# Low part of some weight tiles of the first down projection formed by an accumulating DMA

## The chip, the core and the metric

The kernel runs on one core of a Trainium2 chip. The metric is the device time of one execution in microseconds (us). Five engines work side by side on a core, each with its own queue of instructions in program order, and wait for one another by semaphores: TensorE (PE; the loading of its stationary operand is listed as PEld), VectorE (DVE), ScalarE (ACT), GpSimd (POOL) and SyncE (SP), which here only issues DMAs. Sixteen DMA engines move data between HBM and the on-chip memory SBUF. TensorE accumulates into PSUM.

## The reference

Two layers of a decoder over 256 tokens of width 2048: a retention mixer in layer 0, a convolution module in layer 1, and in each layer a SwiGLU feed-forward and a per-layer embedding, with norms around each. The change touches the last product of the feed-forward of layer 0, `... @ w_down`:

```python
def swiglu(hn, w_gate, w_up, w_down):
    return (jax.nn.silu(hn @ w_gate) * (hn @ w_up)) @ w_down

f = swiglu(rms_norm(h, g_ffn_pre[i]), ffn_w_gate[i], ffn_w_up[i], ffn_w_down[i])
h = h + rms_norm(f, g_ffn_post[i])
```

All data are f32. The hidden width is 5632.

## The kernel before

Every product of activations and weights is computed from parts. A number is split into a high part, its value rounded to TensorE's float32r, and a low part, the number minus the high part. A product is then the sum of three: high by high, high by low and low by high (`mm3`, lines 120 to 122).

`gemm` (line 124) computes a block of 256 tokens by 512 output columns. Tokens are two tiles of 128 (`tt`), each with an accumulator in PSUM. K runs in steps of 256 rows (`su`), and for every step `wload` (line 75) prepares one weight tile of 128 partitions by 2 x 512 numbers, 512 KB:

1. SP loads it into a stage tile `st` (line 68); there are four stage buffers.
2. ACT casts it to the high part `wh` (line 79); there are eight buffers.
3. DVE subtracts, `wl = st - wh` (line 84); there are eight buffers of `wl` too.

PE then does 12 products per tile: two halves of 128 rows, two token tiles, three parts. The engines take tiles in program order, so a cast waits for PE to have finished the tile eight before, and a load waits until the stage tile four before has been read by both ACT and DVE. In the ordinary form of `gemm` both token tiles are served inside the loop over K. With `outer=True` the token tiles are the outer loop and the eight weight tiles stay for both; this form has its own call of `wload` (line 146).

`ffn` (line 565) goes through the hidden width in three groups of 3, 4 and 4 blocks of 512. For each group it computes gate ("fg") and up ("fu") blocks, forms the hidden activations, and then multiplies them with the group's rows of `w_down` ("fd") for each of four blocks `c` of 512 output columns. In a group of four blocks, K of "fd" is 2048: eight weight tiles per block, 32 per group. The results of the second group are added to what is there by DVE (line 601); those of the third go through `make_final` (lines 528 and 530). Only the last block of the third group has `outer=True`.

GpSimd does little: a power of a column of 128 numbers for each norm (`rstd_from`, line 170), and some memsets. No DMA is issued from it.

Of the kernel before, what the change touches and what calls it, by code (L numbers as in the profile page):

```python
# [17 lines left out]
P = 128  # L18
# [11 lines left out]
NFREQ = BLOCK_LEN // 2  # L30
# column offsets of the conv transform's matrices, each as a high and a low part side by side
DFT_AT = {}
# [9 lines left out]
def block_kernel(ctx: ExitStack, tc: tile.TileContext, x, p, positions, w_in, w_out, w_pw1, b_pw1,  # L42
# [15 lines left out]

# [1 line left out]
    def t512(name):  # L60
# [13 lines left out]

    def wload(src, shape=(2, CW)):
        st = stage.tile([P] + list(shape), F32, tag="st", name="st")
        wdma(st, src)
        wh = wpool.tile([P] + list(shape), F32R, tag="wh", name="wh")
        nc.scalar.copy(wh, st)  # L79
        wl = wpool.tile([P] + list(shape), F32R, tag="wl", name="wl")  # L80
        with ExitStack() as es:
            if held:
                es.enter_context(tc.issue_after(held[0].ins))
            nc.vector.tensor_tensor(wl, st, wh.bitcast(F32), op=ALU.subtract)  # L84
        return wh, wl
# [19 lines left out]
    def split_to(act, q, tt, src):  # L105
        """src: [P, 4, 128] f32 (psum or sbuf), channel on partition."""
        hi, lo = act.quarter(q)
        a = nc.scalar.copy(hi[:, tt], src)  # L108
        b = nc.vector.tensor_tensor(lo[:, tt], src, hi[:, tt].bitcast(F32), op=ALU.subtract)  # L109
        return a, b  # L110

    def transpose4(src, n=4):
        """src: [P, n*128] f32 in sbuf -> psum tile [P, n, 128]"""
        tp = tpp.tile([P, n, P], F32, tag="tp", name="tp")
        for j in range(n):
            nc.tensor.transpose(tp[:, j, :], src[:, j * P:(j + 1) * P], ident)
        return tp
# [5 lines left out]

    def gemm(act, w, k0, c0, nkt, name, outer=False, hooks=None, on_done=None, hooks1=None):
        """acc[tt] = act.T @ w[k0:k0+128*nkt, c0:c0+512]"""
        hooks, hooks1 = hooks or {}, hooks1 or {}
        acc = [acc_tile(f"{name}{tt}") for tt in range(TT)]
        if not outer:
            for su in range(nkt // 2):
                wh, wl = wload(wsrc(w, k0 + su * 256, c0))  # L130
                for r in range(2):
                    kt = su * 2 + r
                    for tt in range(TT):
                        xh, xl = act.get(tt, kt)
                        mm3(acc[tt], xh, xl, wh[:, r, :], wl[:, r, :], kt == 0, kt == nkt - 1)
                if su in hooks:
                    hooks[su]()
            if on_done:
                for tt in range(TT):
                    on_done(tt, acc[tt])  # L140
        else:
            ws = []
            for tt in range(TT):
                for su in range(nkt // 2):
                    if tt == 0:
                        ws.append(wload(wsrc(w, k0 + su * 256, c0)))
                    wh, wl = ws[su]
                    for r in range(2):
                        kt = su * 2 + r
                        xh, xl = act.get(tt, kt)  # L150
                        mm3(acc[tt], xh, xl, wh[:, r, :], wl[:, r, :], kt == 0, kt == nkt - 1)
                    at = (hooks, hooks1)[tt]
                    if su in at:
                        at[su]()
                if on_done:
                    on_done(tt, acc[tt])
        return acc

    def rstd_from(ssq, n):
        """ssq: [P, m] partial sums of squares -> [P, 1] rstd"""  # L160
        m = ssq.shape[-1]
        if m > 1:
            s = small.tile([P, 1], F32, tag="s1", name="s1")
            nc.vector.tensor_reduce(s, ssq, axis=mybir.AxisListType.X, op=ALU.add)
        else:
            s = ssq
        v = small.tile([P, 1], F32, tag="s2", name="s2")
        nc.vector.tensor_scalar(v, s, 1.0 / n, EPS, op0=ALU.mult, op1=ALU.add)
        r = small.tile([P, 1], F32, tag="rstd", name="rstd", bufs=8)
        nc.gpsimd.tensor_tensor(r, v, neghalf, op=ALU.pow)  # L170
        return r
# [11 lines left out]

# [1 line left out]
    ident = const.tile([P, P], F32, name="ident")  # L185
# [7 lines left out]
    def preload(func):  # L193
        """has ACT's table loaded ahead of its use"""
        nc.scalar.activation(warm, neghalf, func)

    preload(AF.Silu)

    # what opens the chain comes first: the first gain, then x and the first weights by turns
    cols = const.tile([P, 96], F32, name="cols")  # L200
# [38 lines left out]

# [1 line left out]
    def prenorm_quarter(act, q, tt, src, gcol):  # L241
# [11 lines left out]
    def next_in(engine, i):  # L253
        """keeps an engine to the order in which the opening is traced"""
        if engine in turn:
            tc.add_manual_dep(i.ins, turn[engine].ins.name,
                              mybir.DependencyInfo(mybir.DependencyClass.NoSync, mybir.DependencyReason.DATA),
                              reason="opening")
        turn[engine] = i

    def opening(acc):
        """first product: x is transposed and split by quarters, in step with the weights"""
        fs = {}
# [49 lines left out]
    def rotary_tables():  # L313
# [35 lines left out]
        for a, c in ((a1, cs[2]), (a2, cs[1]), (a2, cs[0]), (a1, cs[1])):  # L349
# [4 lines left out]
            nc.vector.tensor_tensor(tacc, tacc, q, op=ALU.add)  # L354
        # the largest product, up to 2**29, sheds its whole turns in two steps
        nc.vector.tensor_scalar(q, a1, cs[0], None, op0=ALU.mult)
# [102 lines left out]
    def later(f):  # L459
        """behind the opening on DVE"""  # L460
        def g():
            with tc.issue_after(turn["dve"].ins):
                f()
        return g
# [17 lines left out]
    for h in range(HEADS):  # L482
# [15 lines left out]
        gemm(xa, wi, 0, 8192 + CW * h, NKT, "g", hooks=hk2, on_done=hd.g_done)  # L498
        # q and k columns of the head share one accumulator
        acc = [acc_tile(f"qk{tt}") for tt in range(TT)]  # L500
# [11 lines left out]

    # second half of the output projection, post norm and residual
    def post_setup():
        return [ssq_tile() for _ in range(TT)]

    def make_final(c, ssqs, gvec, after, bias=None, first=False):
        """evacuation of the last K group of chunk c; after(tt, rstd) runs at the last chunk"""
        gt = bcast_chunk(gvec, c)
# [43 lines left out]

# [1 line left out]
    def ffn(layer, s_hid, after):  # L565
# [6 lines left out]
        for gi, n in enumerate(groups):  # L572
# [20 lines left out]
            for c in range(NC):  # L593
                last = gi == len(groups) - 1
                if last:
                    done = make_final(c, ssqs, g_ffn_post[layer], after)
                elif gi == 0:
                    done = first_group_done(c)
                else:
                    def done(tt, ps, c=c):  # L600
                        nc.vector.tensor_tensor(y[tt, c], ps, y[tt, c], op=ALU.add)
                gemm(hid, wd, f0 * CW, c * CW, 4 * n, "fd", outer=(last and c == NC - 1),
                     on_done=done, hooks={1: pend} if c == 0 else None)
            f0 += n
        es.close()

    # operand sets: retention 0 and 1, ffn0 0 with hidden 1, ple0 0, conv 1, pw2 0, ffn1 1 with hidden 0, ple1 1
    pa = [Act(0, "pa0"), Act(1, "pa1")]
# [7 lines left out]

# [1 line left out]
    def ple(layer, after):  # L618
# [44 lines left out]

# [1 line left out]
    ca = Act(1, "ca")  # L665
# [11 lines left out]
    def conv(after):  # L677
# [17 lines left out]
        def mm3c(ps, name, rows, hi, lo, first, last):  # L695
            """constant stationary, data moving"""
            nc.tensor.matmul(ps, lhsT=dmat(name, rows, 0), rhs=hi, start=first, stop=False)
# [3 lines left out]
        class Chunk:  # L701
# [26 lines left out]
            def taps(self):  # L728
                """transform of the taps of the chunk's channels"""
                c = self.c  # L730
# [115 lines left out]
def _constants():  # L846
    """tables that depend on shapes alone: rotary frequencies and the decay masks of the heads"""
    inv = (10000.0 ** (-np.arange(P, dtype=np.float64) / P)).astype(np.float32)
# [11 lines left out]
def _short(a):  # L860
    """the nearest numbers of 12 significant bits"""
    m, e = np.frexp(a)
    return np.ldexp(np.rint(m * 4096.0) / 4096.0, e)


def _transform():
    """matrices of an odd-frequency Fourier transform of BLOCK_LEN points, in which the 31 taps and a block of
    128 tokens convolve without wrapping round"""
    th = 2.0 * np.pi * (np.arange(NFREQ) + 0.5) / BLOCK_LEN
# [44 lines left out]
```

## Time and profile before

| | us |
|---|---|
| median of the two runs | 2788.08 |
| the two runs | 2787.88 and 2788.28 |
| span of the profiled execution | 2785.6 |

The span runs from the first to the last instruction of one profiled execution; the time of a run also holds what lies around it. Shares on the profile's page are of the span. A wait is put down to the engine or the DMA whose signal came last. A row `<-` names what a tile is made from or, in a list of waits, who was waited for.

### The profile page before, as it was taken

How to read it: one execution, taken by the hardware profiler on the slowest of the kernel's cores; microseconds unless marked ns; L12 is line 12 of the kernel's file. 1: busy time of each engine (PE TensorE's matmuls, PEld its weight loads, DVE VectorE, ACT ScalarE, POOL GpSimd, SP SyncE). 2: the span in 40 equal slices, each digit the busy share in tenths (PEclk: the TensorE clock that was granted, in tenths of full speed). 3: DMA queues.
4: the chain of work that ended last, by engine and by line, in shares of the span. 5: the costliest groups of instructions: out<-in, count | busy, mean ns of one | idle time of the engine just before them, and what ended most of it. 6: DMA issues, size and time to landing. Idle time of an engine off the chain costs nothing.

```text
span 2785.6 us, 31985 instructions
## 1 busy us (share of the span) xinstructions
PE 2731.3 (98%) x12258; PEld 2251.0 (81%) x12258; DVE 1546.5 (56%) x1673; ACT 1247.0 (45%) x1490; POOL 39.4 (1%) x48
## 2 busy tenths in 40 slices
PE   8999999999999999999999989899999999999998
PEld 7888888888888888888887867668888888888877
DVE  7655545555655445545456566566554455454564
ACT  5444444444454444444445543355444443444453
POOL 0000000000000000000000000000000000000000
PEclk9999999999999999999999999999999999999999
DMA  8655555556565666566555555436655665665553
GB/s 270 192 179 183 182 193 183 181 178 212 169 209 189 195 190 189 189 195 189 190 201 178 179 192 164 154 111 211 214 188 191 193 188 192 191 188 193 202 180 122
DMA packets 288730, 521.76 MB, mean 187 GB/s; under 512 B 17900, under 2 KB 52556, under 8 KB 288576
## 3 DMA queue, kind: packets, MB, share of 16 engines
q1 hardware_dynamic: 288576, 519.71, 57.4%
q8 instruction: 96, 1.57, 0.2%
q14 instruction: 58, 0.48, 0.0%
HBM read 517.55 MB, written 2.10 MB: 187 GB/s over the span
## 4 chain that ended last, share of the span: by engine, by line
PE 92%; DVE 3%; DMA 3%; ACT 1%; issue 0%; POOL 0%; SPq 0%; DVEq 0%; POOLq 0%; ACTq 0%
PE fu L122 6%; PE fu L120 6%; PE fu L121 6%; PE fg L122 6%; PE fg L121 6%; PE fg L120 5%; PE fd L121 5%; PE fd L120 5%; PE fd L122 5%; PE v L121 2%; PE v L122 2%; PE v L120 2%; PE g L120 2%; PE g L122 2%; PE g L121 2%; PE qk L121 2%
## 5 line engine op out<-in xcount | busy, mean ns | idle before, releaser
L84 DVE TENSOR_TENSOR wl<-st,wh 128x1024 fp32r<-128x1024 f32 x944 | 1153.5, 1224 | 1075.4 <-ACT wh L79 1072.9
L79 ACT CAST wh<-st 128x1024 fp32r<-128x1024 f32 x944 | 993.0, 1053 | 1285.0 <-PE fu L122 270.2
L120 PE MATMUL fg<-wh,h_fa 128*128 128x512 f32 x704 | 275.4, 392 | 0.5 <-ACT h_fa L108 0.5
L121 PE MATMUL fg<-wl,h_fa 128*128 128x512 f32 x704 | 274.4, 390 | 0.4 <-DVE wl L84 0.4
L120 PE MATMUL fd<-wh,h_hid 128*128 128x512 f32 x704 | 274.8, 390 | 0.0
L122 PE MATMUL fg<-wh,l_fa 128*128 128x512 f32 x704 | 274.5, 390 | 0.0
L122 PE MATMUL fd<-wh,l_hid 128*128 128x512 f32 x704 | 274.2, 389 | 0.0
L121 PE MATMUL fd<-wl,h_hid 128*128 128x512 f32 x704 | 274.1, 389 | 0.0
L120 PE MATMUL fu<-wh,h_fa 128*128 128x512 f32 x704 | 273.9, 389 | 0.0
L121 PE MATMUL fu<-wl,h_fa 128*128 128x512 f32 x704 | 273.9, 389 | 0.0
L122 PE MATMUL fu<-wh,l_fa 128*128 128x512 f32 x704 | 273.9, 389 | 0.0
L121 PEld LDWEIGHTS fg<-wl,h_fa 128*128 128x128 f32 x704 | 132.2, 188 | 27.9 <-DVE wl L84 1.1
L122 PEld LDWEIGHTS fg<-wh,l_fa 128*128 128x128 f32 x704 | 132.2, 188 | 27.6 <-DVE l_fa L109 0.4
L120 PEld LDWEIGHTS fg<-wh,h_fa 128*128 128x128 f32 x704 | 132.2, 188 | 27.4 <-ACT h_fa L108 0.7
L121 PEld LDWEIGHTS fu<-wl,h_fa 128*128 128x128 f32 x704 | 132.2, 188 | 27.5
L122 PEld LDWEIGHTS fu<-wh,l_fa 128*128 128x128 f32 x704 | 132.2, 188 | 27.4
L122 PEld LDWEIGHTS fd<-wh,l_hid 128*128 128x128 f32 x704 | 132.2, 188 | 27.4
L120 PEld LDWEIGHTS fu<-wh,h_fa 128*128 128x128 f32 x704 | 132.2, 188 | 27.3
L120 PEld LDWEIGHTS fd<-wh,h_hid 128*128 128x128 f32 x704 | 132.2, 188 | 27.2
L121 PEld LDWEIGHTS fd<-wl,h_hid 128*128 128x128 f32 x704 | 132.2, 188 | 27.0
L120 PE MATMUL v<-wh,h_x 128*128 128x512 f32 x256 | 101.0, 396 | 0.0
L121 PE MATMUL v<-wl,h_x 128*128 128x512 f32 x256 | 100.3, 392 | 0.5 <-DVE wl L294 0.5
(235 smaller groups left out, 3819.7 us busy)
## 6 DMA issues: line engine op xcount, KB each, us to landing
st<-in_ffn_w_gate_dram SPq DMA_DIRECT2D x176, 512.0 KB, 3.6
st<-in_ffn_w_up_dram SPq DMA_DIRECT2D x176, 512.0 KB, 3.6
st<-in_ffn_w_down_dram SPq DMA_DIRECT2D x176, 512.0 KB, 3.5
st<-in_ret_w_in_dram SPq DMA_DIRECT2D x128, 512.0 KB, 3.7
st<-in_conv_w_pw_dram SPq DMA_DIRECT2D x96, 512.0 KB, 3.8
st<-in_ret_w_in_dram SPq DMA_DIRECT2D x128, 256.0 KB, 2.8
st<-in_ret_w_out_dram SPq DMA_DIRECT2D x64, 512.0 KB, 3.6
st<-in_ple_w_gate_dram SPq DMA_DIRECT2D x64, 512.0 KB, 4.9
```

Of the source, the lines that this page charges most:

```text
L79: nc.scalar.copy(wh, st)
L84: nc.vector.tensor_tensor(wl, st, wh.bitcast(F32), op=ALU.subtract)
L120: nc.tensor.matmul(ps, lhsT=xh, rhs=wh, start=first, stop=False)
L121: nc.tensor.matmul(ps, lhsT=xh, rhs=wl, start=False, stop=False)
L122: nc.tensor.matmul(ps, lhsT=xl, rhs=wh, start=False, stop=last)
```

## The change

`wload` gets an argument `by_dma`. Where it is set, ACT writes the negative of the stage tile, rounded, into `wl`, and GpSimd issues a DMA that adds to `wl` either the stage tile in SBUF (`"sbuf"`) or once more the weights from HBM (`"dram"`). DVE's subtraction falls away for these tiles. `gemm` passes the flag on for odd `su`, in the ordinary form only. `ffn` sets it for layer 0: nothing in the first group, the stage tile as source in the second, the weights in HBM in the third. The rest of the diff takes away comments and is left out.

```diff
-    def wload(src, shape=(2, CW)):
+    def wload(src, shape=(2, CW), by_dma=None):
         st = stage.tile([P] + list(shape), F32, tag="st", name="st")
         wdma(st, src)
         wh = wpool.tile([P] + list(shape), F32R, tag="wh", name="wh")
         nc.scalar.copy(wh, st)
         wl = wpool.tile([P] + list(shape), F32R, tag="wl", name="wl")
+        if by_dma:
+            nc.scalar.activation(wl, st, AF.Copy, scale=-1.0)
+            nc.gpsimd.dma_start(wl, st if by_dma == "sbuf" else src, accum_op=ALU.add)
+            return wh, wl
         with ExitStack() as es:
...
-    def gemm(act, w, k0, c0, nkt, name, outer=False, hooks=None, on_done=None, hooks1=None):
+    def gemm(act, w, k0, c0, nkt, name, outer=False, hooks=None, on_done=None, hooks1=None, lo_dma=None):
...
-                wh, wl = wload(wsrc(w, k0 + su * 256, c0))
+                wh, wl = wload(wsrc(w, k0 + su * 256, c0), by_dma=lo_dma if su % 2 == 1 else None)
...
                 gemm(hid, wd, f0 * CW, c * CW, 4 * n, "fd", outer=(last and c == NC - 1),
-                     on_done=done, hooks={1: pend} if c == 0 else None)
+                     on_done=done, hooks={1: pend} if c == 0 else None,
+                     lo_dma=(None, "sbuf", "dram")[gi] if layer == 0 else None)
```

## Rows read from the trace of the kernel before

**Rows 1.** The page, part 1: busy us, share of the span, instructions of each engine.

```profile
PE 2731.3 (98%) x12258; PEld 2251.0 (81%) x12258; DVE 1546.5 (56%) x1673; ACT 1247.0 (45%) x1490; POOL 39.4 (1%) x48
```

**Rows 2.** The page, part 4: the chain that ended last, by engine.

```profile
PE 92%; DVE 3%; DMA 3%; ACT 1%; issue 0%; POOL 0%; SPq 0%; DVEq 0%; POOLq 0%; ACTq 0%
```

**Rows 3.** Busy us by stretch: the two down projections that change.

```profile
core 0: us, PE busy (x) PEld busy (x) DVE busy (x) ACT busy (x) POOL busy (x), PEclk, DMA share, GB/s
1136.00:1226.00 90.00, 90.00 (x403) 74.64 (x402) 47.08 (x45) 35.70 (x35) 0.00 (x0) 1.00 0.57 192
1402.00:1494.00 92.00, 91.45 (x416) 75.62 (x415) 53.67 (x60) 40.87 (x53) 1.48 (x1) 1.00 0.53 181
```

**Rows 4.** Waits, 1136 to 1226 us: us in total, times, longest.

```profile
ACT wh L79 <- PE fd L122: 53.2, 32, 1.7
DVE wl L84 <- ACT wh L79: 42.9, 33, 1.5
...
SPq L68 <- DVE wl L84: 73.6, 32, 3.2
```

**Rows 5.** Timeline of ACT: start us, us, instruction, idle time before it.

```profile
1158.58 1.05 ACT L79 CAST wh<-st 128x1024 fp32r<-128x1024 f32 x1 [1.67 <-PE fd L122]
1161.30 1.05 ACT L79 CAST wh<-st 128x1024 fp32r<-128x1024 f32 x1 [1.67 <-PE fd L122]
```

**Rows 6.** Timeline of DVE in the same stretch.

```profile
1158.09 1.28 DVE L601 TENSOR_TENSOR y<-fd,y 128x512 f32<-128x512 f32 x2
1159.67 1.23 DVE L84 TENSOR_TENSOR wl<-st,wh 128x1024 fp32r<-128x1024 f32 x1 [0.30 <-ACT wh L79]
...
1179.85 1.28 DVE L601 TENSOR_TENSOR y<-fd,y 128x512 f32<-128x512 f32 x2
```

**Rows 7.** DMA issues, 1136 to 1226 us: count, size, median us to landing.

```profile
st<-in_ffn_w_down_dram SPq DMA_DIRECT2D x21, 512.0 KB, 3.5
```

**Rows 8.** Groups by line: busy us, mean ns, idle us before, what ended it.

```profile
L84 DVE TENSOR_TENSOR wl<-st,wh 128x1024 fp32r<-128x1024 f32 x944 | 1153.5, 1224 | 1075.4 <-ACT wh L79 1072.9 <-PE pg L122 1.4
L79 ACT CAST wh<-st 128x1024 fp32r<-128x1024 f32 x944 | 993.0, 1053 | 1285.0 <-PE fu L122 270.2 <-PE fd L122 245.4 <-PE fg L122 231.1
```

**Rows 9.** POOL: groups by line; and rstd's shortest, median, longest ns.

```profile
L170 POOL TENSOR_TENSOR rstd<-s,neghalf 128x1 f32<-128x1 f32 x36 | 35.6, 988 | 2502.3 <-DVE s L168 2502.3
...
L899 POOL MEMSET const-float32-0.0<- 128x1 f32 x1 | 0.1, 98 | 0.2 <-issue 0.2
...
L170 POOL TENSOR_TENSOR rstd<-s,neghalf x36: 547/548/3664, 34.8 to 2778.8; 128x1 f32<-128x1 f32 x36
```

**Rows 10.** DMA issues of the whole span, columns as in rows 7.

```profile
st<-in_ret_w_in_dram SPq DMA_DIRECT2D x128, 512.0 KB, 3.7
...
st<-in_ret_w_in_dram SPq DMA_DIRECT2D x128, 256.0 KB, 2.8
...
st<-in_ple_w_gate_dram SPq DMA_DIRECT2D x64, 512.0 KB, 4.9
...
out_dram<-h SPq DMA_DIRECT2D x8, 256.0 KB, 2.5
...
g<-in_conv_b_dw_dram SPq DMA_DIRECT2D x4, 256.0 KB, 10.7
```

## The prediction

> **What bounds the kernel now.** I read the busy line of the page first, then the chain that ended last, then the stretch that the change touches. TensorE (PE) is busy 98% of the span [rows 1] and carries 92% of the chain [rows 2]. In layer 0 the second group's down projection is multiplied between about 1136 and 1226 us, the third group's between 1402 and 1494 us. PE is busy for 90.00 of 90.00 us in the first and 91.45 of 92.00 us in the second, at a granted clock of 1.00, its level of 2.4 GHz [rows 3]. So there is nothing to win here unless PE has to do less, and PE's work is not touched. What is open is whether it can be made to wait.
>
> The waits of the first stretch tell who is ahead of whom. ACT's cast waits for PE 32 times, 1.67 us each (53.2 us), and VectorE (DVE) waits for ACT's cast 33 times, 1.3 us each [rows 4]. The preparation of weights therefore stands still until PE gives a buffer back: it runs as far ahead as the eight buffers of wh and wl allow. The loads in turn wait for DVE's subtraction, which frees a stage buffer (73.6 us in 32 waits) [rows 4].
>
> Two distances follow. Casts start 2.72 us apart [rows 5], which is PE's time for one tile. The cast at 1158.58 starts when PE has finished the last tile of a block: the block's results are taken up by DVE at 1158.09, and those of the next block at 1179.85, 21.76 us = 8 x 2.72 us later [rows 5, 6]. The tile cast at 1158.58 is the eighth after the one just finished, so PE comes to it 7 x 2.72 = 19.0 us after the start of its cast. DVE's subtraction for it runs from 1159.67 to 1160.90 [rows 6], 2.32 us after that start: wl has 16.7 us to spare. The second distance is the stage buffer's turn. There are four, so a buffer is needed again 4 x 2.72 = 10.88 us after its cast started. It is free 2.32 us into this turn, and the load takes 3.5 us from issue to landing [rows 7], so 5.0 us are spare.
>
> **The change, part by part.** The flag is passed only in the branch that loops over K with both token tiles inside, for odd su. The second group gives 4 blocks x 4 = 16 tiles with the stage tile as source; the third gives 3 x 4 = 12 with the weights in HBM as source, since its last block goes through the outer branch. I count 28 tiles rather than the 32 of the short description; nothing below turns on the difference of four.
>
> Removed: 28 subtractions on DVE at 1.22 us [rows 8] = 34 us. DVE waited 42.9 us of 90 us in the first stretch already [rows 4]; on the path this is worth 0.
>
> Added on ACT: 28 copies with scale -1 from the same tile to a tile of the same type as the cast, taken at the cast's 1.05 us [rows 8] = 29.5 us. ACT's gap before a cast is 1.67 us [rows 4, 5], so one more instruction of 1.05 us on every second tile fits in the gap. Cost 0; without the gap it would only use up some of the 16.7 us by which wl is ahead.
>
> Added on POOL: 28 DMA issues, each behind ACT's copy. POOL is idle in the first stretch [rows 3] and nothing of this layer that PE awaits stands behind these issues in its queue until the rstd of the last block. Moved past other queues: SP's loads of a stage buffer used as source now wait for the accumulating DMA to land, not for DVE; SP issues in order, so a late load delays the next one too.
>
> Unknown is L, the time from the end of ACT's copy until the sum has landed: POOL's issue p and the transfer X. No row shows either. For p the nearest rows are POOL's own: 0.10 us for its smallest instruction, 0.99 us mean and 3.66 us longest for rstd [rows 9]. For X they are transfers of SP: 2.5 us for 256 KB stored, 2.8 us for 256 KB loaded, 3.7 us for 512 KB of the same matrix, and 10.7 us the longest median [rows 10]. The two loads give 0.9 us for each further 256 KB. One stream of 512 KB would take 3.7 us; but the addition has to read the destination as well as the source, 1024 KB, and the second stream adds 2 x 0.9 us: 5.5 us. I take p = 1.0 us, the mean on the same engine, and X = 5.5 us: L = 6.5 us. The bounds are 2.6 us (0.10 + 2.5) and 14.4 us (3.66 + 10.7).
>
> The Trainium skill, page "Collectives: The Full Stack", section "The bandwidth ceiling: the fold count and why AG ≠ RS ≠ AR", speaks against the change: a reduction in the DMA path runs at half the rate of a copy because it reads two sources. No row here shows an accumulation. By a plain copy's 3.7 us L would be 4.7 us, and by two streams 6.5 us; the sums below hold either.
>
> Price for the 12 tiles with HBM as source. ACT's copy ends 2.1 us after the cast starts and wl is wanted at 19.0 us: L may be 16.9 us. Both bounds fit, so 0, as long as several such DMAs can be under way. The stage buffer is free at 2.1 us, not later than before.
>
> Price for the 16 tiles with the stage tile as source. The slot's turn is 2.1 + L + 3.5 us and must not exceed 10.88 us, so L may be 5.3 us. At 6.5 us each turn is late by 1.2 us. Su is odd for the same two of the four slots every time; each has 8 turns, and before the last such tile 7 of them count: 7 x 1.2 = 8.6 us. Against that stands the lead of wl, 16.9 - 6.5 = 10.4 us. The lateness is eaten by the lead and PE never waits: 0. In general PE loses 7(L - 5.27) - (16.9 - L) = 8L - 53.8 us, which is above zero from L = 6.7 us on. With the lower bound nothing is late; with the upper it is 61 us. My value lies close under the point where it begins to cost, and that decides the range.
>
> Sum: 0 - 34 us of DVE off the path, + 29.5 us of ACT in its gaps, + 28 transfers within the lead = 0 us. The profiled execution's span of 2785.6 us stays; the two timed runs have their median 2.5 us above it at 2788.08, so 2788.1 us.
>
> **The rivals.**
> *Slots turn too slowly.* L lies above 6.7 us, or the loads themselves get longer beside the new traffic. For it: loads that crowd have a median of 4.9 us [rows 10]; at 4.9 instead of 3.5 us the slot's allowance falls to 3.9 us and the loss becomes 8L - 44, or 8 us at L = 6.5. Against: the DMA engines are busy only 57% [rows 3]. With L = 8 to 11 us the first formula gives 10 to 34 us. Time: 2790 to 2825, and up to 2844 at the edge of 2%.
> The Trainium skill, page "DMA: Bandwidth & Descriptors", section "Queues, rings and completion order", says that each DMA engine takes packets from its queues by turns, so that a load would share with an accumulation under way. No row of one queue shows this.
>
> *One accumulation at a time, slower by over 2%.* The place is POOL's queue: if the next such DMA starts only when the last has landed, or if the transfers fill the engines, one is delivered every L and one is wanted every 2 x 2.72 = 5.44 us. The loss is 15(L - 5.44) - (16.9 - L) in the first stretch and 11(L - 5.44) - (16.9 - L) in the second, together 28L - 175 us. It passes 2% (55.8 us) at L = 8.3 us; at 10 us it is 105 us, that is 2893 us. In the engines' terms: two loads take 57% of 5.44 us, 1.55 us each, and 2.3 us are free for an accumulation, 1.5 times a load. For it: the two streams and the row at 10.7 us. Against: SP's loads do overlap, landing after 3.5 us while issued every 2.72 us [rows 7], and 8.3 us would be well above twice a load.
>
> *A gain.* DVE's 34 us could matter only where PE waits, and in these stretches PE is idle 0.55 us altogether [rows 3]: 2787.5 us at best.
>
> **How the numbers follow.** Hidden, within 2 us of before: 0.58. Slots too slow: 0.25. Over 2%: 0.15. A gain of any size: 0.02. The likeliest gives 2788 us. A range from 2786 to 2825 us leaves out the third, and of the second what lies above L = 11 us (about 0.04), and so holds about 0.8; the hidden case alone would be 2786 to 2790. Faster by over 2%, which is about what a measurement of this kernel tells from no change, has no place to come from: 0.01. Slower by over 2%: 0.15. Within: 0.84.
>
> **What would show it.** Right: PE busy without a gap in the same two stretches, DVE with 28 subtractions fewer, ACT with 28 more instructions of about 1.05 us, a POOL queue of DMAs of 512 KB landing within about 7 us. Wrong: PE waiting for wl by a DMA at L121, SP's loads waiting for a DMA rather than for DVE, casts that wait for the load of st, or landing times above 7 us in the first stretch; PE waits in the second stretch alone would speak for one at a time.

## The result and the profile after

The changed kernel takes 2810.98 us against 2788.08 us, a ratio of 1.0075 with a 95% interval of [1.0056, 1.0094]: 22.9 us slower. (The quotient of the two medians is 1.0082, in the same interval.) The profiled execution grew as much, from a span of 2785.6 to 2808.3 us.

The page of the kernel after, first part 1, then part 4, the chain by engine:

```profile
PE 2740.3 (98%) x12258; PEld 2254.7 (80%) x12258; DVE 1512.1 (54%) x1645; ACT 1271.2 (45%) x1518; POOL 68.3 (2%) x76
...
PE 82%; issue 9%; DVE 3%; DMA 3%; ACT 1%; POOL 1%; SPq 0%; POOLq 0%; DVEq 0%; ACTq 0%
```

DVE has 28 instructions fewer and ACT 28 more, as counted. The chain, 92% PE before [rows 2], now lies for 9% in "issue": an engine that waits for nothing that the profile shows. These 9%, some 250 us, are not the loss. The longest piece, from the chain in order of time (start us, us, what), is

```profile
1215.14 171.09 issue
```

In it POOL has nothing to do between the two groups, and PE is busy all the while, 176.00 of 176.00 us between 1226 and 1402 us. The stretches tell where the loss lies (columns as in [rows 3]; the second one is longer, since the same work now ends later):

```profile
1136.00:1226.00 90.00, 90.00 (x403) 74.64 (x402) 27.44 (x28) 43.96 (x47) 11.42 (x13) 1.00 0.96 265
...
1402.00:1520.00 118.00, 102.69 (x434) 81.79 (x432) 46.59 (x56) 50.40 (x64) 14.17 (x12) 0.96 0.74 201
```

In the second group, where the stage tile is the source, PE is busy for 90.00 of 90.00 us, as before. The whole loss lies in the third group, where HBM is the source: PE idles for 15.3 us of 118, against 0.55 us of 92 before [rows 3]. (Before, the 95.3 us up to 1497.3, 22.7 us less than 118, have 0.55 us of idle time too.) The waits between 1376 and 1520 us, in total, times and longest:

```profile
POOL wl L83 <- issue: 50.4, 7, 9.0
...
POOL wl L83 <- ACT wh L79: 28.0, 4, 8.7
...
PE fd L125 <- DMA wl<-in_ffn_w_down_dram: 14.2, 7, 4.1
```

PE waits for wl, wl for its DMA, and the DMA was issued late by POOL, which sat idle before it without a cause that the profile names. Four of its waits are put down to a cast of ACT (28.0 us); but ACT's copy for the tile, which POOL does need, had ended long before in each. The timelines of three engines give the cause. First ACT's second copy, then POOL's issues, then PE's waits in the same stretch:

```profile
1390.17 1.06 ACT L82 ACTIVATE wl<-st 128x1024 fp32r<-128x1024 f32 x1 [1.44 <-PE fu L125]
```

```profile
1386.24 1.22 POOL L83 DMA_DIRECT2D wl<-in_ffn_w_down_dram  x1 [171.10 <-ACT wl L82]
1395.80 1.23 POOL L83 DMA_DIRECT2D wl<-in_ffn_w_down_dram  x1 [8.34 <-issue]
1405.60 1.20 POOL L83 DMA_DIRECT2D wl<-in_ffn_w_down_dram  x1 [8.57 <-ACT wh L79]
...
1454.75 1.20 POOL L83 DMA_DIRECT2D wl<-in_ffn_w_down_dram  x1 [8.06 <-issue]
...
1471.64 1.20 POOL L83 DMA_DIRECT2D wl<-in_ffn_w_down_dram  x1 [8.99 <-issue]
1477.94 1.22 POOL L83 DMA_DIRECT2D wl<-in_ffn_w_down_dram  x1 [5.10 <-issue]
```

```profile
1454.47 0.50 PE L125 MATMUL fd<-wl,h_hid 128*128 128x512 f32 x1 [3.54 <-DMA wl<-in_ffn_w_down_dram]
1471.36 0.50 PE L125 MATMUL fd<-wl,h_hid 128*128 128x512 f32 x1 [4.09 <-DMA wl<-in_ffn_w_down_dram]
```

ACT's copy for the second tile is done at 1391.23, but POOL issues at 1395.80. Where PE shows the landing of one accumulation (1454.47, 1471.36), POOL issues the next 0.28 us later (1454.75, 1471.64). The landing times of the single DMAs say the same of all: the second took 9.5 us and so landed at 1405.3, and the third was issued at 1405.60; each of the eleven later issues comes 0.3 to 0.4 us after the landing before it. One accumulation at a time: twelve issues take 91.7 us from first to last, 8.34 us each, and PE wants one every 5.44 us.

### The profile page after: what moved, and what is told of

It is laid out like the page before. It is cut to its first block, busy times and chain, and to the rows that moved or that the text cites. A ratio compares the mean times of both kernels' runs of the same rounds, so it can differ in the third digit from the quotient of the medians.

```text
span 2808.3 us, 32054 instructions
## 1 busy us (share of the span) xinstructions
PE 2740.3 (98%) x12258; PEld 2254.7 (80%) x12258; DVE 1512.1 (54%) x1645; ACT 1271.2 (45%) x1518; POOL 68.3 (2%) x76
## 4 chain that ended last, share of the span: by engine, by line
PE 82%; issue 9%; DVE 3%; DMA 3%; ACT 1%; POOL 1%; SPq 0%; POOLq 0%; DVEq 0%; ACTq 0%
PE fu L125 5%; PE fu L126 5%; PE fu L124 5%; PE fd L125 4%; PE fd L126 4%; PE fg L125 4%; PE fg L126 4%; PE fd L124 4%; PE fg L124 4%; PE v L125 2%; PE v L126 2%; PE v L124 2%; PE g L124 2%; PE g L126 2%; PE qk L124 2%
## 5 line engine op out<-in xcount | busy, mean ns | idle before, releaser
L88 DVE TENSOR_TENSOR wl<-st,wh 128x1024 fp32r<-128x1024 f32 x916 | 1118.5, 1224 | 1117.1 <-ACT wh L79 1115.7
```

## The experiments

Theory A, formed from these rows: POOL issues an accumulation from HBM only when the one before has landed, because the room for the descriptors of its DMAs holds one of them and not two; the SBUF-sourced ones need less room. The rivals, named in the expectations, put the loss on full DMA engines, on HBM as a source, on lateness carried over from the second group, or on each transfer by itself. Ratios are to the kernel before, run on the same chip beside each set; its own median there was 2789.4, 2792.8 and 2791.0 us in the three sets.

**The two groups apart.**

```diff
-                     lo_dma=(None, "sbuf", "dram")[gi] if layer == 0 else None)
+                     lo_dma=(None, "sbuf", None)[gi] if layer == 0 else None)     # first run
+                     lo_dma=(None, None, "dram")[gi] if layer == 0 else None)     # second run
```

> Only the second group's 16 tiles go by DMA, with the stage tile as source; the third group is made by VectorE as before. Theory A (the loss is all in the third group, because POOL issues an accumulation with HBM as source only when the one before has landed): 2788 us, within 2 us of before, PE busy 90.0 of 90.0 us between 1136 and 1226 us. Rival B (both groups cost, through DMA engines that are 96% busy in the second group's stretch, and the lateness of the second group is carried into the third): 2792 to 2800 us, with PE waiting after 1226 us.

> Only the third group's 12 tiles go by DMA, with HBM as source; the second group is made by VectorE. Theory A: the whole loss, 2811 us, with POOL's issues about 8.3 us apart. Rival B (lateness carried over from the second group): less than the whole, 2797 to 2805 us.

The second group alone: 2791.4 us, ratio 1.0004 [0.9995, 1.0014]. The third alone: 2812.1 us, ratio 1.0075 [1.0058, 1.0092], the whole loss. Nothing is carried over.

**More room for descriptors.**

```diff
-    nc = bacc.Bacc("TRN2", target_bir_lowering=False, num_devices=1, dynamic_dma_scratch_size=1024)
+    nc = bacc.Bacc("TRN2", target_bir_lowering=False, num_devices=1, dynamic_dma_scratch_size=1920)   # and 1536
```

> The changed kernel, with 1920 instead of 1024 bytes per partition set aside for the descriptors of POOL's DMAs; nothing else differs. Theory A in the form that it is the room for descriptors that holds POOL back: a second HBM accumulation can be under way, POOL issues within about 0.3 us of ACT's copy, issues 5.44 us apart on average, and the loss goes: 2788 to 2791 us. Rival C (the DMA engines are full: share 0.91 at issues 8.3 us apart, so more transfers under way only land later): the landing time rises from 7.7 to 12 us or more, the rate stays at one in about 8 us, 2808 to 2811 us. Rival D (POOL waits for the landing of each HBM accumulation whatever its room): nothing changes, 2811 us.

> As the run with 1920 bytes for descriptors, but with 1536, half as much again as in the changed kernel. Theory A: there is room for two HBM accumulations (one took more than half of 1024 bytes), two under way at 9 us landing give one per 4.5 us, less than the 5.44 us wanted, so the loss goes as with 1920: 2788 to 2793 us. If one transfer took more than 768 bytes, nothing changes: 2811 us.

With 1920 bytes 2792.0 us, 1.0009 [0.9999, 1.0018]; with 1536 bytes 2791.4 us, 0.9993 [0.9984, 1.0002]. One number outside the computation takes the loss away. With 1920 bytes POOL's timeline and the DMA row (count, KB, median us to landing) read:

```profile
1385.32 1.22 POOL L83 DMA_DIRECT2D wl<-in_ffn_w_down_dram  x1 [171.31 <-ACT wl L82]
1390.86 1.21 POOL L83 DMA_DIRECT2D wl<-in_ffn_w_down_dram  x1 [4.32 <-ACT wl L82]
```

```profile
wl<-in_ffn_w_down_dram POOLq DMA_DIRECT2D x12, 512.0 KB, 9.0
```

Now each issue is released by ACT's copy, 5.4 us after the one before, while that one still needs 3.6 us to land. A landing got longer, 9.0 instead of 7.7 us, and the time shorter. That answers rivals C and D. The stretch of 1390 to 1450 us in this run (columns as in [rows 3]):

```profile
1390.00:1450.00 60.00, 60.00 (x270) 49.78 (x269) 20.98 (x23) 36.05 (x43) 13.23 (x11) 1.00 1.07 290
```

PE does not wait although the share of the DMA engines is 1.07. A share can thus pass 1, and one near 1 does not by itself mean that something waits for the engines.

**The stage tile as source in both groups.**

```diff
-                     lo_dma=(None, "sbuf", "dram")[gi] if layer == 0 else None)
+                     lo_dma=(None, "sbuf", "sbuf")[gi] if layer == 0 else None)
```

> Both groups take the stage tile as source, so the third group's 12 tiles too. Theory A: the loss goes, because these DMAs are issued at once and take 5.2 us to land: 2788 us, within 2 us. Rival C (any further accumulation beside the third group's loads and its final evacuation is too much): PE waits between 1402 and 1500 us, 2795 us or more.

2790.9 us, 1.0000 [0.9990, 1.0009]. The 28 accumulations are hidden where the source is the stage tile, and the third group's stretch is not special. Their landing, from the DMA row of this run:

```profile
wl<-st POOLq DMA_DIRECT2D x28, 512.0 KB, 5.1
```

**Pieces or HBM.** The two sources differ in where they lie and in how many pieces they come: a partition of the stage tile is one run of 4 KB, a row of the tile in HBM is 2 KB. The queue's packets show it: the run with the second group alone has 2304 for 16 transfers, 144 each, the run with the third alone 3264 for 12, 272 each.

```diff
+    def src4():
+        return w_down[0][0:P, 0:2 * CW].rearrange("p (t n) -> p t n", t=2)
...
-            nc.gpsimd.dma_start(wl, st if by_dma == "sbuf" else src, accum_op=ALU.add)
+            nc.gpsimd.dma_start(wl, st if by_dma == "sbuf" else src4(), accum_op=ALU.add)
```

> The changed kernel, but the accumulation in the third group adds 128 whole rows of 4 KB from the start of the weights in HBM instead of 256 row pieces of 2 KB of the tile's own rows: the same 512 KB from HBM in half as many pieces. The sums are then wrong numbers (the data added are other weights); the work is the same. Theory A (room counted in pieces: one transfer of 256 pieces fills the room, one of 128 does not): POOL issues right behind ACT's copy, 5.4 us apart, some less than a landing time apart; 2788 to 2792 us. Rival D (any accumulation with HBM as source waits for the one before): POOL still waits with the copy done; if the landing stays near 7.7 us the time stays at 2805 to 2811 us, if it falls to 5 us the wait stays but the time falls to 2790 us.

> The run with 4 KB rows from HBM once more, for a profile (the profile of the first was taken in an execution of 7058 us; as there, the sums are wrong numbers, the work is the same). Theory A: some of POOL's issues in the third group are less than a landing time apart, none waits with ACT's copy done, PE does not wait in the stretch; landing below the 9.0 us of the 2 KB pieces with room. Rival D: each issue comes only after the landing of the one before.

2791.6 us, the median of eight executions, 0.9994 [0.9984, 1.0004]. Two more took 7058 and 8464 us; in the first, which has a trace, a product of "fg" lasts 0.83 us instead of 0.39. Why was not found, and both are left out. The run made once more took 2788.9 us and gives the rows:

```profile
q0 software_dynamic: 4032, 14.68, 2.8%
...
wl<-in_ffn_w_down_dram POOLq DMA_DIRECT2D x12, 512.0 KB, 8.0
```

```profile
1384.67 0.88 POOL L86 DMA_DIRECT2D wl<-in_ffn_w_down_dram  x1 [171.59 <-ACT wl L85]
1390.11 0.88 POOL L86 DMA_DIRECT2D wl<-in_ffn_w_down_dram  x1 [4.56 <-ACT wl L85]
```

4032 packets for 28 transfers are 144 each. With 1024 bytes of room, HBM as source and 8.0 us to land, POOL issues every 5.4 us and PE does not wait. So it is the number of pieces, not HBM, that let only one transfer be under way.

The pieces can also be halved by making the transfer smaller:

```diff
-            nc.gpsimd.dma_start(wl, st if by_dma == "sbuf" else src, accum_op=ALU.add)
+            for r in range(1 if by_dma == "sbuf" else 2):
+                if by_dma == "sbuf":
+                    nc.gpsimd.dma_start(wl, st, accum_op=ALU.add)
+                else:
+                    nc.gpsimd.dma_start(wl[:, r], src[:, r], accum_op=ALU.add)
```

> The changed kernel, but each accumulation from HBM is issued as two DMAs of 256 KB, one for each half of the tile, 128 pieces of 2 KB each. Theory A (room counted in pieces): two halves fit where one whole did, the second is issued at once, the next tile's first half as soon as one half has landed; PE waits less but not never: 2792 to 2808 us. Rival D (one DMA with HBM as source at a time, whatever its size): the halves follow each other, landing time twice per tile, 2811 us or more.

2793.3 us, 0.9998 [0.9988, 1.0007]: at the lower end of the 2792 to 2808 us expected, and better in that PE never waits for wl. The timeline of POOL in this run shows how far the room goes:

```profile
1386.86 1.79 POOL L87 DMA_DIRECT2D wl<-in_ffn_w_down_dram  x2 [170.48 <-ACT wl L82]
1392.30 0.90 POOL L87 DMA_DIRECT2D wl<-in_ffn_w_down_dram  x1 [3.65 <-ACT wl L82]
1394.45 0.89 POOL L87 DMA_DIRECT2D wl<-in_ffn_w_down_dram  x1 [1.25 <-issue]
```

The first half lands 7.3 us after its issue, at 1394.2. The third half is issued at 1392.30 with two still under way; the fourth waits until 1394.45, 0.3 us after the first has landed. So 1024 bytes hold three halves of 144 packets (the queue has 5760 in all, 2304 of them the second group's) and not four (432, not 576), and not two wholes of 272 (544). A row of halves closes the gap that wholes leave, and the rate suffices.

**Less room, with the stage tile as source.**

```diff
-                     lo_dma=(None, "sbuf", "dram")[gi] if layer == 0 else None)
+                     lo_dma=(None, "sbuf", None)[gi] if layer == 0 else None)
...
-    nc = bacc.Bacc("TRN2", target_bir_lowering=False, num_devices=1, dynamic_dma_scratch_size=1024)
+    nc = bacc.Bacc("TRN2", target_bir_lowering=False, num_devices=1, dynamic_dma_scratch_size=512)
```

> Only the second group by DMA, from the stage tile, with 512 instead of 1024 bytes for descriptors. Theory A: half the room holds one of these transfers, so they too are issued one at a time, 0.3 us after the landing of the one before, never 2.9 us apart as in the changed kernel. One lands in 5.2 us, so one per 5.5 us against 5.44 us wanted: the lead covers it and nothing is lost, 2788 to 2793 us. If standing one behind another costs by itself, 2800 us or more. If the issues still come 2.9 us apart, the room is not what theory A says.

2829.8 us, 1.0141 [1.0126, 1.0157]: 39 us slower, where I expected at most a few; of the three cases named, "standing one behind another costs by itself" is the one that came. Against the run of the second group alone (2791.4 us) only the constant differs. The order of events was as theory A has it: each issue after the first comes 0.2 to 0.4 us after the landing before it. The size was missed. The stretch of 1136 to 1226 us (columns as in [rows 3]), POOL's timeline and the DMA rows of the stretch:

```profile
1136.00:1226.00 90.00, 73.06 (x294) 57.47 (x293) 16.40 (x17) 30.80 (x32) 8.85 (x10) 0.92 0.73 178
```

```profile
1143.67 0.90 POOL L83 DMA_DIRECT2D wl<-st  x1 [7.98 <-ACT wh L79]
1152.44 0.88 POOL L83 DMA_DIRECT2D wl<-st  x1 [7.87 <-ACT wh L79]
```

```profile
st<-in_ffn_w_down_dram SPq DMA_DIRECT2D x20, 512.0 KB, 7.3
wl<-st POOLq DMA_DIRECT2D x10, 512.0 KB, 8.5
```

The landing is 8.5 us here and 5.2 us in the changed kernel, for the same transfer. A landing now releases two things at once: the stage buffer, on which SP issues two loads (from 1143.40), and the room, on which POOL issues the next accumulation (1143.67). The three run side by side, the loads' landing grows to 7.3 us [rows 7: 3.5], and between the rounds the DMA engines have little to do (share 0.31 from 1151.00 to 1152.40 us, 0.21 from 1143.60 to 1145.00). That the lockstep alone sets the 8.5 us was read from these rows, not tried. With 8.8 us from issue to issue, the formula of the prediction's second rival for the first stretch, 16L - 98.5, gives 42 us if 8.8 us are put in the place of L; measured are 39.

The Trainium skill, page "DMA: Bandwidth & Descriptors", section "Queues, rings and completion order", has each DMA engine take packets from its queues by turns; loads of 7.3 us beside an accumulation agree with that.

**The rate.**

```diff
-                wh, wl = wload(wsrc(w, k0 + su * 256, c0), by_dma=lo_dma if su % 2 == 1 else None)
+                wh, wl = wload(wsrc(w, k0 + su * 256, c0), by_dma=lo_dma if su % (4 if lo_dma == "dram" else 2) == 1 else None)
```

> The changed kernel, but in the third group every fourth tile is added from HBM, not every second: 6 instead of 12, the other 6 by VectorE. Theory A in its rate form (one in 8.3 us can be delivered, one in 10.9 us is wanted): no loss at all, 2788 to 2792 us, POOL never waits with the copy done. Rival E (each of these transfers costs its share, 22.9 us / 12 = 1.9 us): 2799 to 2802 us.

2790.9 us, 0.9999 [0.9989, 1.0009]. With one wanted every 10.9 us and 9.4 us to land, nothing is lost. Six of these transfers cost 0 and twelve 22.9 us: it is a rate that is exceeded, not a price for each.

**All 32 tiles of the second group.**

```diff
-                wh, wl = wload(wsrc(w, k0 + su * 256, c0), by_dma=lo_dma if su % 2 == 1 else None)
+                wh, wl = wload(wsrc(w, k0 + su * 256, c0), by_dma=lo_dma if su % 2 == 1 or lo_dma == "sbuf" else None)
...
-                     lo_dma=(None, "sbuf", "dram")[gi] if layer == 0 else None)
+                     lo_dma=(None, "sbuf", None)[gi] if layer == 0 else None)
```

> All 32 tiles of the second group are added by DMA from the stage tile, not every second one; the third group is made by VectorE. By the slot's turn alone (2.1 + 6.3 + 3.5 = 11.9 us against 10.88, 7 turns late by 1.0 us, lead 10 us) nothing is lost: 2788 us. By the DMA engines' share (96% busy with one accumulation for two loads: 1.55 us a load, 2.1 us an accumulation, so 3.65 us for each tile of 2.72 us, 32 x 0.93 us less the lead of 10 us) the loss is 20 us: 2808 us, with PE waiting for wl between 1160 and 1240 us.

2817.8 us, 1.0089 [1.0074, 1.0105]: 25 us against 20 from the engines' share and 0 from the slot's turn. The same stretch, PE's wait between 1100 and 1530 us, and the DMA rows of the stretch:

```profile
1136.00:1226.00 90.00, 76.75 (x317) 58.50 (x315) 5.42 (x8) 45.83 (x48) 20.18 (x23) 0.98 1.04 259
```

```profile
PE fd L125 <- DMA wl<-st: 19.9, 18, 3.1
```

```profile
wl<-st POOLq DMA_DIRECT2D x23, 512.0 KB, 7.7
st<-in_ffn_w_down_dram SPq DMA_DIRECT2D x22, 512.0 KB, 5.7
```

That the engines' share came near does not confirm it; its price of an accumulation was too low, as shown below. The slot's turn was worked out with shorter times; with those measured here it is 2.1 + 7.7 + 5.7 = 15.5 us, for four slots 3.9 us per tile, and the 32 issues come 4.0 us apart (from 1117.21 to 1241.06 us). SP waits for a landing to free a slot in 83.5 of the 90 us. So the tiles come as fast as the slots turn, and the turn is slow because an accumulation lands after 7.7 us, not 5.2, and a load after 5.7, not 3.5 [rows 7]. Whether the DMA engines are the bound, which is rival C for one accumulation to every load, stays open: their share is 1.04 here, but 1.07 in the run with 1920 bytes, where PE does not wait.

## Why the prediction was wrong

The step that failed is the price of the 12 tiles from HBM. It ran: both bounds of L fit into 16.9 us, "so 0, as long as several such DMAs can be under way". The latency did fit: 7.7 us, 9.9 us at most. The condition did not hold. It had been written down and then put at 0.15 among the rivals, with SP's overlapping loads [rows 7] as the evidence against it. Those rows speak of SP's queue. Of POOL's queue no row of before could speak, and the one number in the code that bears on it, `dynamic_dma_scratch_size=1024` in the kernel's last function, was not weighed.

The rival "one accumulation at a time" was the right mechanism in half of its place. I applied it to both groups, with one L, as 28L - 175. Only the term of the second stretch holds, 11(L - 5.44) - (16.9 - L) = 12L - 76.7: with the measured L = 8.34 us it gives 23.4 us, and the span grew by 22.7. Because the 16 other tiles need half the room, the sum fell far below the 2% that this rival was priced at. The time lies inside the range only because another rival stretched it there; the rival "slots turn too slowly" was not what happened.

The other steps, in their order:

- *PE is the bound, DVE's 34 us are worth nothing.* Right. In the runs without the loss DVE does up to 28 subtractions less and the ratio is 1.00.
- *ACT's copies fit in its gaps.* Right: ACT is busy for 43.96 us of 90 in the first stretch, and PE does not wait.
- *L = 6.5 us for the stage tile.* Measured from the end of ACT's copy (1143.53 + 1.06) to the issue (1144.94) and the landing 5.0 us later: 5.4 us. The landing already holds POOL's 0.9 us of issue, so p was counted on top where it is inside; X with the second stream, 5.5 us, was near. What it cost the DMA engines is in their queues' rows of 1136 to 1226 us (packets, MB, the packets' time as a share of 16 engines; below them the loads, with their landing):

```profile
q1 hardware_dynamic: 8679, 16.75, 52.8%
q0 software_dynamic: 1944, 7.05, 42.9%
...
st<-in_ffn_w_down_dram SPq DMA_DIRECT2D x24, 512.0 KB, 6.0
```

1944 packets are 13.5 accumulations of 144, 0.429 x 90 / 13.5 = 2.9 us each; 8679 are 31.9 loads, if a load has 272 packets as the 512 KB in rows of 2 KB above, 0.528 x 90 / 31.9 = 1.5 us each. By this estimate an accumulation takes 1.9 times a load, and the 2.1 us that I used in the expectation for all 32 tiles was too little: it assumed one accumulation every 5.44 us, 16.5 in a stretch that held 13.5. The Trainium skill ("Collectives: The Full Stack", section "The bandwidth ceiling: the fold count and why AG ≠ RS ≠ AR") gives the halved rate for the reduction step of a ring of collectives. The packets' time of this DMA agrees with it, 2.9 against 1.5 us; the landing does not show it, 5.2 us against 3.5 [rows 7].
- *Slots are late, and wl's lead eats the lateness.* Right. The stretch's last accumulation, issued at 1214.26, landed at 1219.0, and PE came to that tile about 2.5 us later. The prediction left 10.4 - 8.6 = 1.8 us. The loads did get longer, 6.0 us in this stretch [rows 7: 3.5]; with them the slot's allowance is 10.88 - 2.1 - 6.0 = 2.8 us and the prediction's formula becomes 8L - 36.4, 7 us of loss at L = 5.4, and none was seen, so it overstates.
- *What would show it.* "PE waits in the second stretch alone would speak for one at a time" was the sign that came.

Not all of the 22.7 us is PE waiting. PE idles 15.3 - 0.55 = 14.8 us more, and behind some of its waits it runs slower. By stretches of 20 us, and for 3 us behind the wait of 4.09 us above (columns as in [rows 3]):

```profile
1400.00:1420.00 20.00, 20.00 (x94) 16.66 (x93) 7.16 (x8) 11.85 (x13) 2.41 (x2) 1.00 0.91 256
1420.00:1440.00 20.00, 15.76 (x61) 11.88 (x60) 5.82 (x7) 8.53 (x12) 3.40 (x3) 0.91 0.91 231
1440.00:1460.00 20.00, 15.72 (x61) 12.20 (x60) 4.45 (x5) 7.47 (x8) 2.62 (x3) 0.91 0.85 214
1460.00:1480.00 20.00, 15.91 (x64) 12.68 (x63) 6.71 (x7) 7.00 (x10) 3.63 (x3) 0.91 0.73 179
...
1472.51:1475.50 2.99, 2.99 (x8) 2.31 (x7) 0.00 (x0) 0.00 (x0) 0.32 (x1) 0.50 0.78 129
```

```profile
1472.94 0.63 PE L124 MATMUL fd<-wh,h_hid 128*128 128x512 f32 x1
1473.37 0.63 PE L125 MATMUL fd<-wl,h_hid 128*128 128x512 f32 x1
```

Until 1420 us PE is busy without a gap at a granted clock of 1.00, its 2.4 GHz level. In the 60 us from there on the mean is 0.91: behind three of the waits, those of 2.32, 3.54 and 4.09 us, products start 0.43 us apart for some 3.5 us, at a granted clock of 0.50, the 1.2 GHz level. Between these three stretches it is 1.00 again. In these 60 us 186 products took 47.4 us; at 2.72 / 12 = 0.227 us each they would have taken 42.2. So about 5 us are the clock's and 15 us the waits'. The product behind the down projection starts 21.7 us later than before (1512.5 against 1490.8 us), so 1 us of the remaining 3 arises only behind it; the other 2 I can't assign. The formula 12L - 76.7 holds both kinds of loss: it asks only how late the last accumulation lands.

## What to carry to other kernels

A transfer that is late by less than its lead costs nothing; ask instead how many of them can be under way at once, in that queue, and divide. Where a queue's room is set by a constant in the code, work out what one transfer takes of it: fewer and longer runs per transfer, a smaller transfer or a larger constant each took the whole loss away here. And evidence that one queue overlaps its transfers says nothing of another queue.

## What the runs showed that I had not expected

- POOL holds a DMA back until there is room for it, and the profile calls that wait "issue" or puts it down to a later cast of ACT. 1024 bytes per partition held three transfers of 144 packets or one of 272; 1536 bytes held two of 272; 512 bytes one of 144. The Trainium skill, page "DMA: Bandwidth & Descriptors", section "SWDGE vs HWDGE vs iDMA", places the descriptors of POOL's DMAs in rings in SBUF; that a larger reserve lets more DMAs be under way agrees.
- The same accumulation of 512 KB lands after 4.7 to 7.8 us in one arrangement and after 5.7 to 9.2 us, with a median of 8.5, in another. What the landing before it releases is the likely reason, read from the rows and not tried.
- Serialising can cost more than the sum of the pieces suggests: 39 us in the run with 512 bytes, with a share of the DMA engines of 0.73 in the stretch, less than the 0.96 of the changed kernel, which loses nothing there.
